# Instance norm in 3D: tiles of 48 KiB per partition in four slots, with masked sums and some stores on the load queue

## The chip, the core and the metric

The kernel runs on one core of a Trainium2 chip. Five engines are used: VectorE (DVE), ScalarE (ACT), TensorE (PE), GpSimd (POOL) for the set-up, and SyncE (SP), which issues loads. Transfers between HBM and the on-chip memory (SBUF, 128 partitions) are issued on queues of SP and ACT and carried by 16 DMA engines that all queues share. The metric is the device time of one execution in microseconds, as the median of the runs; less is better.

## The reference

Each of 8 x 64 = 512 instances (one batch entry and one channel) has 32 x 64 x 64 = 131072 float32 values. Each is normalised by its own mean and variance:

```
mean = np.mean(x, axis=(2, 3, 4), keepdims=True)
var = np.var(x, axis=(2, 3, 4), keepdims=True)
return ((x - mean) / np.sqrt(var + eps)).astype(np.float32)
```

The input is 268.4 MB, and so is the output; each value must be read once and written once.

## The kernel before

**Tiles.** A tile is 128 partitions x 8192 columns, 32 KiB per partition, 4 MiB, contiguous in HBM. It holds 8 instances, 16 partitions each. There are 64 tiles; the last is taken as two halves of 4096 columns per partition. Six tile buffers (`slots`) of 32 KiB per partition take turns: tile k is in slot k % 6. `LANES` = 8 sets of semaphores, small buffers and PSUM banks serve six slots and two halves.

**Engines.** Every engine has its own instruction stream, written out in order; semaphores connect them, and there is no scheduler. `over_tiles` runs one engine's `step` over ten rounds of six tiles (a hardware loop) and then over the rest, three tiles and two halves. For one tile:

- `on_vector` (DVE): sums the left half of the columns (L79), later adds the two sums out of PSUM with the sign turned, which is minus the mean (L82), takes the reciprocal of the root (L89), makes the shift (L92), and scales and shifts the right half in place (L95).
- `on_scalar` (ACT): sums the right half (L107), squares the whole tile around the mean with a running sum (L113), takes the root of the variance plus eps (L120), scales and shifts the left half in place (L123), and issues the store of the tile (L130) when both halves are done.
- `on_tensor` (PE): two matmuls with a constant 128 x 128 matrix `avg` that adds the 16 partitions of an instance and divides by 131072 (L136 for the sums, L143 for the squares).

The outputs of L107 and L113 themselves are thrown away (`unused`, one byte per element); only their sums count.

**Queues.** `load_all` (SP) issues six loads at once (L180); then, in a loop, the load of each further tile waits until the store of the tile that had the slot has landed (L185, and L192 for the rest). All stores are on ACT's queue, behind the work of their tile in ACT's stream. A queue's transfers are carried in order of issue. At the end ACT waits for all stores.

**Set-up.** GpSimd builds `avg` (for 8 and for 4 instances) with a memset (L201) and masks (L204), and the constant eps (L214); ACT and PE wait for it.

Of the kernel before, what the change touches and what calls it, by code (L numbers as in the profile page):

```python
# [9 lines left out]
def kernel(  # L10
# [17 lines left out]
    COLS = 8192  # L28
    SLOTS = 6
    FULL = P * COLS // n_elem  # L30
    n_tiles = n_inst // FULL
    ROUNDS = (n_tiles - 1) // SLOTS
    LANES = SLOTS + 2

    x_f = x.rearrange("b c d h w -> (b c) (d h w)")
    out_f = out.rearrange("b c d h w -> (b c) (d h w)")
    x_t = x_f.rearrange("(k i) (s f) -> k (i s) f", i=FULL, s=P // FULL)
    out_t = out_f.rearrange("(k i) (s f) -> k (i s) f", i=FULL, s=P // FULL)
    x_h = x_f.rearrange("(k i) (s f) -> k (i s) f", i=FULL // 2, s=2 * P // FULL)
    out_h = out_f.rearrange("(k i) (s f) -> k (i s) f", i=FULL // 2, s=2 * P // FULL)  # L40

    ctx.enter_context(tc.tile_critical(name="norm"))  # L42

    def sbuf(name, shape, dtype=fp32):
# [4 lines left out]
    unused = sbuf("unused", [P, COLS], mybir.dt.uint8)  # L49
    eps_t = sbuf("eps_t", [P, 1])  # L50
    avg = {n: sbuf(f"avg{n}", [P, P]) for n in (FULL, FULL // 2)}
    small = [sbuf(f"small{i}", [P, 8]) for i in range(LANES)]
    psum = [
        ctx.enter_context(nc.psum_tensor(f"psum{i}", [P, 512], fp32))
        for i in range(LANES)
    ]

    def semaphores(name, n):
        return [ctx.enter_context(nc.semaphore(f"{name}{i}")) for i in range(n)]

    ready = semaphores("ready", 1)[0]
    landed = semaphores("landed", LANES)
    summed = semaphores("summed", LANES)
    meaned = semaphores("meaned", LANES)
    centred = semaphores("centred", LANES)
    squared = semaphores("squared", LANES)
    varied = semaphores("varied", LANES)
    rooted = semaphores("rooted", LANES)
    scaled = semaphores("scaled", LANES)
    shifted = semaphores("shifted", LANES)  # L70
    done = semaphores("done", LANES)
    stored = semaphores("stored", LANES)
# [3 lines left out]
    def on_vector(eng, t, lane, n, c1, c2, c16):  # L76
        w = t.shape[1] // 2
        a = small[lane]
        eng.reduce_sum(  # L79
            out=a[:, 0:1], in_=t[:, :w], axis=mybir.AxisListType.X  # L80
        )._wait_ge(landed[lane], c16).then_inc(summed[lane], 1)
        eng.tensor_reduce(  # L82
            out=a[:, 2:3],
            in_=psum[lane][:, 0:2],
            axis=mybir.AxisListType.X,
            op=Alu.add,
            negate=True,
        )._wait_ge(meaned[lane], c1).then_inc(centred[lane], 1)
        eng.reciprocal(out=a[:, 5:6], in_=a[:, 4:5])._wait_ge(  # L89
            rooted[lane], c1  # L90
        ).then_inc(scaled[lane], 1)
        eng.tensor_mul(out=a[:, 6:7], in0=a[:, 2:3], in1=a[:, 5:6])._wait_ge(  # L92
            scaled[lane], c1
# [4 lines left out]
            scalar1=a[:, 5:6],  # L98
            scalar2=a[:, 6:7],
            op0=Alu.mult,  # L100
            op1=Alu.add,
        )._wait_ge(shifted[lane], c1).then_inc(done[lane], 1)

    def on_scalar(eng, t, lane, n, c1, c2, c16, dst):
        w = t.shape[1] // 2
        a = small[lane]
        eng.activation(  # L107
            out=unused[:, w : 2 * w],
            in_=t[:, w:],
            func=Act.Identity,  # L110
            accum_out=a[:, 1:2],
        )._wait_ge(landed[lane], c16).then_inc(summed[lane], 1)
        eng.activation(  # L113
            out=unused[:, : 2 * w],
# [4 lines left out]
        )._wait_ge(centred[lane], c1).then_inc(squared[lane], 1)  # L119
# [7 lines left out]
            scale=a[:, 5:6],  # L127
            bias=a[:, 6:7],
        )._wait_ge(shifted[lane], c1).then_inc(done[lane], 1)
        eng.dma_start(out=dst, in_=t)._wait_ge(done[lane], c2).then_inc(  # L130
            stored[lane], 16
        )

# [131 lines left out]
```

## Time and profile before

| what | value |
|---|---|
| median of 3 runs | 1248.04 us (1247.95 to 1248.22) |
| the profiled execution: its own time | 1247.95 us |
| its span in the profile | 1246.2 us |
| instructions in the span | 1808 |
| bytes moved | 536.90 MB, 431 GB/s over the span |
| share of the chain that ended last | ACT 48%, DVE 29% |
| DVE's idle time before L79, ended by a load | 163.7 us in 53 waits |
| ACT's idle time before L107, ended by a load | 76.7 us in 44 waits |
| activation table loads | 20, of 1283 ns each |

The page has the busy time of each engine, the span in 40 slices (a digit is the busy share in tenths), the DMA queues with their packets (q1 carries what SP issues, q10 what ACT issues), the chain of work that ended last, the groups of instructions by line, and the DMA issues with their time to landing. In a group the shape is out<-in, then the count, busy time and the mean of one, and the idle time before them with what ended it. Idle time of an engine that does not set the end costs nothing.

### The profile page before, as it was taken

How to read it: one execution, taken by the hardware profiler on the slowest of the kernel's cores; microseconds unless marked ns; L12 is line 12 of the kernel's file. 1: busy time of each engine (PE TensorE's matmuls, PEld its weight loads, DVE VectorE, ACT ScalarE, POOL GpSimd, SP SyncE). 2: the span in 40 equal slices, each digit the busy share in tenths (PEclk: the TensorE clock that was granted, in tenths of full speed). 3: DMA queues.
4: the chain of work that ended last, by engine and by line, in shares of the span. 5: the costliest groups of instructions: out<-in, count | busy, mean ns of one | idle time of the engine just before them, and what ended most of it. 6: DMA issues, size and time to landing. Idle time of an engine off the chain costs nothing.

```text
span 1246.2 us, 1808 instructions
## 1 busy us (share of the span) xinstructions
PE 76.4 (6%) x260; PEld 65.2 (5%) x260; DVE 468.0 (38%) x325; ACT 986.1 (79%) x410; POOL 1.9 (0%) x11
## 2 busy tenths in 40 slices
PE   0000000000000000000000000000000000000000
PEld 0000000000000000000000000000000000000000
DVE  2344334433334334343343433434334333343331
ACT  5888888887787878778777877787787778878774
POOL 0000000000000000000000000000000000000000
DMA  9999999999999999999999999999999999999998
GB/s 404 421 438 428 430 438 436 428 431 438 435 429 431 438 435 429 431 436 436 429 431 436 436 429 430 438 436 426 433 438 436 426 433 438 435 425 435 438 429 380
DMA packets 18722, 536.90 MB, mean 431 GB/s; under 512 B 2080, under 2 KB 2080, under 8 KB 2080
## 3 DMA queue, kind: packets, MB, share of 16 engines
q1 hardware_dynamic: 9360, 268.44, 50.0%
q10 hardware_dynamic: 9360, 268.44, 49.9%
q14 instruction: 2, 0.02, 0.0%
HBM read 268.44 MB, written 268.44 MB: 431 GB/s over the span
## 4 chain that ended last, share of the span: by engine, by line
ACT 48%; DVE 29%; another core or an unknown queue 13%; PE 6%; issue 1%; DMA 1%; ACTq 0%; DVEq 0%; SPq 0%
ACT unused L113 37%; DVE small L79 18%; DVE slot L95 8%; ACT slot L123 4%; ACT unused L107 4%; PE psum L136 3%; PE psum L143 3%; ACT small L120 1%; ACT L120 1%; DMA slot<-in_x_dram 1%; DVE small L89 1%; DVE small L82 1%; DVE small L92 1%; ACTq L130 0%
## 5 line engine op out<-in xcount | busy, mean ns | idle before, releaser
L113 ACT ACTIVATE unused<-slot,small 128x8192 uint8<-128x8192 f32 (+1 forms) x65 | 456.1, 7016 | 90.2 <-DVE small L82 90.2
L79 DVE TENSOR_REDUCE small<-slot 128x1 f32<-128x4096 f32 (+1 forms) x65 | 283.0, 4353 | 163.7 <-DMA slot<-in_x_dram 163.7
L107 ACT ACTIVATE unused<-slot 128x4096 uint8<-128x4096 f32 (+1 forms) x65 | 231.7, 3564 | 81.9 <-DMA slot<-in_x_dram 76.7
L123 ACT ACTIVATE slot<-slot,small 128x4096 f32<-128x4096 f32 (+1 forms) x65 | 243.7, 3749 | 27.6 <-DVE small L92 27.6
L89 DVE RECIPROCAL small<-small 128x1 f32<-128x1 f32 x65 | 10.6, 164 | 533.8 <-ACT small L120 533.8
L95 DVE TENSOR_SCALAR slot<-slot,small 128x4096 f32<-128x4096 f32 (+1 forms) x65 | 154.7, 2380 | 2.4
L136 PE MATMUL psum<-small,avg 128*128 128x2 f32 x130 | 38.2, 363 | 673.9 <-DVE small L79 548.5
L136 PEld LDWEIGHTS psum<-small,avg 128*128 128x128 f32 x130 | 32.6, 311 | 679.4 <-DVE small L79 552.7
L143 PE MATMUL psum<-small,avg 128*128 128x1 f32 x130 | 38.2, 363 | 480.6 <-ACT unused L113 480.6
L143 PEld LDWEIGHTS psum<-small,avg 128*128 128x128 f32 x130 | 32.7, 312 | 486.1 <-ACT unused L113 486.1
L120 ACT ACTIVATE small<-psum,eps_t 128x1 f32<-128x1 f32 x65 | 17.0, 261 | 37.4 <-PE psum L143 37.3
L82 DVE TENSOR_REDUCE small<-psum 128x1 f32<-128x2 f32 x65 | 10.4, 160 | 62.8 <-PE psum L136 62.8
L107 ACT ACT_TABLE_LOAD x10 | 12.8, 1283 | 10.4 <-ACT slot L123 7.1
L120 ACT ACT_TABLE_LOAD x10 | 12.8, 1283 | 0.2
L107 ACT ACTIVATION_READ_ACCUMULATOR unused<-slot 128x1 f32 x65 | 12.1, 186 | 0.0
L113 ACT ACTIVATION_READ_ACCUMULATOR unused<-slot,small 128x1 f32 x65 | 12.1, 186 | 0.0
L92 DVE TENSOR_TENSOR small<-small 128x1 f32<-128x1 f32 x65 | 10.4, 159 | 2.2
L204 POOL TENSOR_SCALAR_AFFINE_SELECT avg<-avg 128x128 f32<-128x128 f32 x4 | 1.3, 324 | 0.3
L201 POOL MEMSET avg<- 128x128 f32 x2 | 0.4, 204 | 0.5 <-SPq L42 0.5
L246 POOL MEMSET const-bfloat16-1.0<- 128x1 bf16 x1 | 0.1, 101 | 0.0
L246 POOL MEMSET const-uint8-127<- 128x1 uint8 x1 | 0.1, 101 | 0.0
L214 POOL MEMSET eps_t<- 128x1 f32 x1 | 0.1, 99 | 0.0
(2 smaller groups left out, 0.2 us busy)
## 6 DMA issues: line engine op xcount, KB each, us to landing
slot<-in_x_dram SPq DMA_DIRECT2D x63, 4096.0 KB, 53.3
out_dram<-slot ACTq DMA_DIRECT2D x63, 4096.0 KB, 45.3
slot<-in_x_dram SPq DMA_DIRECT2D x2, 2048.0 KB, 55.6
out_dram<-slot ACTq DMA_DIRECT2D x2, 2048.0 KB, 14.7
```

Source lines behind the costliest of these rows:

```text
L79: eng.reduce_sum(out=a[:, 0:1], in_=t[:, :w], axis=mybir.AxisListType.X)._wait_ge(landed[lane], c16).then_inc(summed[lane], 1)
L82: eng.tensor_reduce(out=a[:, 2:3], in_=psum[lane][:, 0:2], axis=mybir.AxisListType.X, op=Alu.add, negate=True,)._wait_ge(meaned[lane], c1) ...
L89: eng.reciprocal(out=a[:, 5:6], in_=a[:, 4:5])._wait_ge(rooted[lane], c1).then_inc(scaled[lane], 1)
L92: eng.tensor_mul(out=a[:, 6:7], in0=a[:, 2:3], in1=a[:, 5:6])._wait_ge(scaled[lane], c1).then_inc(shifted[lane], 1)
L95: eng.tensor_scalar(out=t[:, w:], in0=t[:, w:], scalar1=a[:, 5:6], scalar2=a[:, 6:7], op0=Alu.mult, op1=Alu.add,)._wait_ge(shifted[lane], ...
L107: eng.activation(out=unused[:, w : 2 * w], in_=t[:, w:], func=Act.Identity, accum_out=a[:, 1:2],)._wait_ge(landed[lane], c16).then_inc(sum ...
L113: eng.activation(out=unused[:, : 2 * w], in_=t, func=Act.Square, bias=a[:, 2:3], accum_out=a[:, 3:4],)._wait_ge(centred[lane], c1).then_in ...
L120: eng.activation(out=a[:, 4:5], in_=psum[lane][:, 2:3], func=Act.Sqrt, bias=eps_t[:, 0:1])._wait_ge(varied[lane], c1).then_inc(rooted[lane ...
L123: eng.activation(out=t[:, :w], in_=t[:, :w], func=Act.Identity, scale=a[:, 5:6], bias=a[:, 6:7],)._wait_ge(shifted[lane], c1).then_inc(don ...
L136: eng.matmul(out=psum[lane][:, 0:2], lhsT=avg[n][:], rhs=a[:, 0:2], start=True, stop=True,)._wait_ge(summed[lane], c2).then_inc(meaned[lan ...
L143: eng.matmul(out=psum[lane][:, 2:3], lhsT=avg[n][:], rhs=a[:, 3:4], start=True, stop=True,)._wait_ge(squared[lane], c1).then_inc(varied[la ...
L204: eng.affine_select(out=m[:], in_=m[:], pattern=[[sign * split, n], [0, split]], compare_op=Alu.is_ge, fill=0.0, base=0 if sign < 0 else s ...
```

## The change

Tiles become 12288 columns wide, 48 KiB per partition and 6 MiB, in four slots. A tile is made of three chunks of 4096 columns. Since an instance is 32 chunks, a partition can hold the end of one instance and the start of the next. 512 instances are 128 parts of 128 x 4096 columns; two parts (2 MiB each) come first, then 41 tiles, then three parts.

- **Sums by masks.** Each chunk has its own sum. `over_instance` turns the sums per chunk into sums per instance: DVE multiplies the sums of a partition's chunks with a mask `belongs` (which chunk belongs to which of up to three groups of the partition), PE adds over partitions with `avg`, DVE reduces out of PSUM, multiplies with the mask again and reduces, which gives a value per chunk. This is done twice for a tile, for the means and for the variances.
- **Work of a tile.** DVE sums the first chunk and the last 1536 columns; ACT sums the second chunk and 2560 columns of the third. DVE subtracts the mean from the first chunk in place and squares and sums it in one instruction; ACT squares and sums the other two. DVE scales chunk 0 and scales and shifts chunk 1; ACT does chunk 2.
- **Parts.** A part is worked as a half tile was before (`part_on_vector`, `part_on_scalar`, `part_on_tensor`), without a store on ACT.
- **Queues.** On SP: two part loads, the load of tile 0, the store of part 0, the load of tile 1, the store of part 1, the loads of tiles 2 and 3 (which wait for the stores of the parts that lay in their slots), and then the loop. At the end SP issues the load of tile 40, three part loads (into the three chunks of one slot, after the store of tile 37), the store of tile 40 and the stores of the three parts, and waits for all stores. Tiles 0 to 39 are stored on ACT's queue as before.
- **Set-up.** GpSimd builds `within` and `belongs` besides `avg` (for one size); DVE waits for it too. ACT loads the activation table that has the root once, ahead of all.

The diff, cut to its core:

```diff
-    COLS = 8192
-    SLOTS = 6
-    FULL = P * COLS // n_elem
-    n_tiles = n_inst // FULL
-    ROUNDS = (n_tiles - 1) // SLOTS
-    LANES = SLOTS + 2
+    CHUNK = 4096
+    THIRDS = 3
+    COLS = THIRDS * CHUNK
+    SLOTS = 4
+    PART = P * CHUNK // n_elem
+    FRONT = 2
+    n_tiles = (n_inst // PART - FRONT) // THIRDS - 1
+    n_parts = n_inst // PART - THIRDS * n_tiles
+    ROUNDS = n_tiles // SLOTS
+    LANES = SLOTS + n_parts
...
+    def over_instance(eng, a, p, at, m, to, negate, c1, wait, steps):
+        n = THIRDS
+        by_both = at + m
+        by_instance = by_both + n * m
+        by_chunk = by_instance + n
+        eng.tensor_tensor(
+            out=block(a, by_both, n, m),
+            in0=spread(a, at, m),
+            in1=belongs[:, :, :m],
+            op=Alu.mult,
+        )._wait_ge(*wait).then_inc(steps[0], 1)
         eng.tensor_reduce(
...
+            out=a[:, by_instance : by_instance + n],
+            in_=p.rearrange("p (n m) -> p n m", m=m),
+            axis=AXIS,
             op=Alu.add,
...
+        )._wait_ge(steps[1], c1).then_inc(steps[2], 1)
+        eng.tensor_tensor(
+            out=block(a, by_chunk, n, n),
+            in0=spread(a, by_instance, n),
+            in1=belongs[:, :, :n].rearrange("p i c -> p c i"),
+            op=Alu.mult,
+        )._wait_ge(steps[2], c1).then_inc(steps[3], 1)
+        eng.tensor_reduce(
+            out=a[:, to : to + n],
+            in_=block(a, by_chunk, n, n),
+            axis=AXIS,
+            op=Alu.add,
+            negate=negate,
+        )._wait_ge(steps[3], c1).then_inc(steps[4], 1)
...
+    def tile_on_vector(eng, t, lane, c1, c3, c4, c16):
+        a, p = small[lane], psum[lane]
+        chunk = [t[:, i * CHUNK : (i + 1) * CHUNK] for i in range(THIRDS)]
+        for j, part in ((0, chunk[0]), (3, t[:, COLS - TURN :])):
+            eng.reduce_sum(out=column(a, SUMS, j), in_=part, axis=AXIS)._wait_ge(
+                landed[lane], c16
+            ).then_inc(summed[lane], 1)
+        over_instance(
+            eng, a, p[:, 0:12], SUMS, 4, MEANS, True, c1, (summed[lane], c4),
+            (sorted_[lane], meaned[lane], joined[lane], picked[lane], centred[lane]),
+        )
+        eng.tensor_scalar(
+            out=chunk[0],
+            in0=chunk[0],
+            scalar1=column(a, MEANS, 0),
+            scalar2=None,
+            op0=Alu.add,
+        )._wait_ge(centred[lane], c1).then_inc(moved[lane], 1)
+        eng.tensor_tensor_reduce(
+            out=unused[2][:],
+            in0=chunk[0],
+            in1=chunk[0],
+            scale=1.0,
+            scalar=0.0,
+            op0=Alu.mult,
+            op1=Alu.add,
+            accum_out=column(a, SQUARES, 0),
+        )._wait_ge(moved[lane], c1).then_inc(squared[lane], 1)
+        over_instance(
+            eng, a, p[:, 12:21], SQUARES, 3, VARS, False, c1, (squared[lane], c3),
...
+    def tile_on_scalar(eng, t, lane, c1, c3, c4, c16, dst):
...
+        for j, part in ((1, chunk[1]), (2, chunk[2][:, : CHUNK - TURN])):
+            eng.activation(
+                out=unused[j - 1][:, : part.shape[1]],
+                in_=part,
+                func=Act.Identity,
+                accum_out=column(a, SUMS, j),
+            )._wait_ge(landed[lane], c16).then_inc(summed[lane], 1)
+        for j in (1, 2):
+            eng.activation(
+                out=unused[j - 1][:],
+                in_=chunk[j],
+                func=Act.Square,
+                bias=column(a, MEANS, j),
+                accum_out=column(a, SQUARES, j),
+            )._wait_ge(centred[lane], c1).then_inc(squared[lane], 1)
...
+        if dst is not None:
+            eng.dma_start(out=dst, in_=t)._wait_ge(done[lane], c3).then_inc(
+                stored[lane], 16
+            )
...
     def load_all(eng):
+        def part(m):
+            lane, t, slot, uses = parts[m]
+            load = eng.dma_start(out=t, in_=part_of(x_f, m))
+            if uses:
+                load._wait_ge(stored[slot], 16 * uses)
+            load.then_inc(landed[lane], 16)
+
+        def store_part(m):
+            lane, t, _, _ = parts[m]
+            eng.dma_start(out=part_of(out_f, m), in_=t)._wait_ge(done[lane], 2).then_inc(
+                stored[lane], 16
+            )
+        for m in range(FRONT):
+            part(m)
         for s in range(SLOTS):
-            eng.dma_start(out=slots[s][:], in_=x_t[s]).then_inc(landed[s], 16)
+            load = eng.dma_start(out=slots[s][:], in_=x_t[s])
+            if s >= SLOTS - FRONT:
+                load._wait_ge(stored[s + FRONT], 16)
+            load.then_inc(landed[s], 16)
+            if s < FRONT:
+                store_part(s)
...
+        for k in range(ROUNDS * SLOTS, n_tiles):
+            eng.dma_start(out=slots[k % SLOTS][:], in_=x_t[k])._wait_ge(
+                stored[k % SLOTS], 16 * (k // SLOTS)
+            ).then_inc(landed[k % SLOTS], 16)
+        for m in range(FRONT, n_parts):
+            part(m)
+        s = TAIL % SLOTS
+        eng.dma_start(out=out_t[TAIL], in_=slots[s][:])._wait_ge(
+            done[s], 3 * (TAIL // SLOTS + 1)
+        ).then_inc(stored[s], 16)
+        for m in range(FRONT, n_parts):
+            store_part(m)
...
+    nc.vector.wait_ge(ready, set_by)
...
+    nc.scalar.preload_act_table(Act.Sqrt)
     nc.scalar.wait_ge(ready, set_by)
```

`TURN` is 1536, `TAIL` is 40 (the last tile), and `parts` lists lane, buffer, slot and the slot's stores to wait for, for each of the five parts. `block`, `spread` and `column` are views of a small buffer of 72 columns per lane. The two halves of `over_instance` use semaphores of their own.

## The prediction

> **What bounds the kernel now.** I read the page first: busy shares, the 40 slices, the DMA queues.
>
> ```profile
> PE 76.4 (6%) x260; PEld 65.2 (5%) x260; DVE 468.0 (38%) x325; ACT 986.1 (79%) x410; POOL 1.9 (0%) x11
> DMA  9999999999999999999999999999999999999998
> GB/s 404 421 438 428 430 438 436 428 431 438 435 429 431 438 435 429 431 436 436 429 431 436 436 429 430 438 436 426 433 438 436 426 433 438 435 425 435 438 429 380
> q1 hardware_dynamic: 9360, 268.44, 50.0%
> q10 hardware_dynamic: 9360, 268.44, 49.9%
> ```
>
> ScalarE (ACT) is busy 79% of the span, but the two DMA queues together fill 99.9% of the 16 DMA engines' time. Each queue has 63 x 128 packets of 32 KiB (one per partition of a tile), 2 x 128 of 16 KiB and 65 x 16 small packets that close a transfer: 9360.
>
> Next the windows, to see whether the mix of loads and stores matters. Columns: stretch, its length, five engines' busy time, clock, DMA share, GB/s.
>
> ```profile
> 6.00:30.20 24.20, 1.18 (x4) 1.01 (x4) 7.36 (x6) 14.92 (x7) 0.00 (x0) 1.00 1.00 433
> 200.00:1168.25 968.25, 59.11 (x202) 50.55 (x202) 365.70 (x250) 772.32 (x318) 0.00 (x0) 1.00 1.00 433
> 1236.00:1242.07 6.07, 0.00 (x0) 0.00 (x0) 0.00 (x0) 0.00 (x0) 0.00 (x0) 1.00 1.01 432
> ```
>
> Loads alone, both directions, and 16 KiB stores alone all give 432 to 433 GB/s. One queue fills the engines as well as two do. So the end is set by bytes, plus what a packet costs beyond its bytes, plus any time in which neither queue has work.
>
> Last the queues: the issues (size, median us to landing) and the loads' waits.
>
> ```profile
> slot<-in_x_dram SPq DMA_DIRECT2D x63, 4096.0 KB, 53.3
> out_dram<-slot ACTq DMA_DIRECT2D x63, 4096.0 KB, 45.3
> SPq L185 <- DMA out_dram<-slot: 1048.9, 54, 50.6
> ```
>
> Loads wait for free slots, not slots for loads. A tile's load and store take 19.4 us of the engines, and a load lands 53.3 us after its issue, so 34 us of other work stands before it. 53.3 + 45.3 + some 17.5 us of compute is 116 us, six slots at 19.4.
>
> **DMA work, the term that counts.** Bytes stay at 536.87 MB. In the trace's packet records, followed start to start on one DMA engine, a 32 KiB packet takes 1.2094 us and a 16 KiB packet 0.6073. The difference, 0.6021 us, is what 16 KiB cost; 5.2 ns are left per packet. By the windows' rounded rates that remainder lies between 0 and 6 ns. A 48 KiB packet is not in the trace; on the same line it takes 1.8115.
>
> Before, an engine has 63 x 8 x 2 = 1008 large and 32 small data packets. After, it has 41 x 8 x 2 = 656 of 48 KiB and 5 x 8 x 2 = 80 of 16 KiB: 304 fewer, at 5.2 ns, -1.58 us (0 to -1.82 by the windows). Closing packets fall from 130 to 92. On an ordinary engine the records show 6 ns for one, -0.23 us. But a transfer is complete when its slowest engine is, and tiles start every 19.39 us (L107 at 1135.94 and 1155.33 in the timeline), while 16 x 1.2094 is 19.35: 0.04 us per pair of transfers. Nineteen pairs fewer at that price are -0.76. I take -0.5, the middle. Sum -2.1 us, if the engines stay filled.
>
> The Trainium skill, "DMA: Bandwidth & Descriptors", section "Why small descriptors are slow (HBM only)", gives a fixed cost of about 3 cycles per packet and dates it to this chip; with the page's 850 MHz that is an estimate of 3.5 ns, 304 of them are 1.07 us, and the time would be 1246.5 by it. The records' 5.2 ns decide.
>
> **Compute, which must stay inside 29.0 us per tile.** A 48 KiB tile needs 16 x 1.8115 + 0.04 = 29.0 us of the engines. The rows, by form (busy us, mean ns):
>
> ```profile
> L113 ACT ACTIVATE unused<-slot,small 128x4096 uint8<-128x4096 f32 x2 | 7.4, 3707 | 2.0 <-DVE small L82 2.0
> L79 DVE TENSOR_REDUCE small<-slot 128x1 f32<-128x4096 f32 x63 | 278.4, 4419 | 162.0 <-DMA slot<-in_x_dram 162.0
> L79 DVE TENSOR_REDUCE small<-slot 128x1 f32<-128x2048 f32 x2 | 4.6, 2282 | 1.7 <-DMA slot<-in_x_dram 1.7
> L123 ACT ACTIVATE slot<-slot,small 128x4096 f32<-128x4096 f32 x63 | 239.5, 3801 | 26.8 <-DVE small L92 26.8
> L107 ACT ACTIVATE unused<-slot 128x4096 uint8<-128x4096 f32 x63 | 227.8, 3617 | 80.5 <-DMA slot<-in_x_dram 75.8 <-ACT slot L123 4.6
> L107 ACT ACTIVATE unused<-slot 128x2048 uint8<-128x2048 f32 x2 | 3.8, 1910 | 1.3 <-DMA slot<-in_x_dram 0.9 <-ACT slot L123 0.4
> L95 DVE TENSOR_SCALAR slot<-slot,small 128x4096 f32<-128x4096 f32 x63 | 152.0, 2413 | 2.3
> ```
>
> Sums: ACT 3.62 for the middle chunk, 1.91 + 512 x 0.833 ns = 2.34 for 2560 columns, two accumulator reads at 0.19: 6.33. VectorE (DVE) 4.42 + (2.28 - 512 x 1.043 ns) = 6.17. Group step: product, matmul, two reductions, product: four small ops at 0.16 (L82, L92), 0.68 for the matmul (the idle time before L82), some 0.2 of handovers: 1.5. Centred squares: ACT 2 x (3.71 + 0.19) = 7.79; DVE subtracts in 2.41, then the fused square and sum. No such row exists. Below it cannot be under the 2.41 of L95; above, two passes of L79, 8.84. It reads and accumulates as L79 does, so 4.42 + 0.19: 7.0 in all, under ACT. Second group step 1.5, Sqrt 0.3, reciprocal and product 0.36, two DVE scalings 4.83 (ACT's 3.80 beside them), store issue 0.34, further handovers 0.4. Sum 23.4 us; at the upper bound 27.0; at the lower 23.4 still. All are under 29.0, so the sums by masks cost nothing as long as the DMA covers them: the cover is 5.6 us, and without it every us is paid 41 times. The 20 table loads that go (1.28 us each) and the lighter ACT pay nothing either, for the same reason.
>
> **Slots.** Four at 29.0 give the same 116 us. Load 29.0, compute 23.4 and store 29.0 at half rate leave 34 us of queueing (before: 116 - 38.8 - 17.5 = 60). Thinner, but neither queue empties.
>
> **The moved stores and the start.** On SP, two part loads, tile 0's load, then the store of part 0, which waits for its result; behind it in SP stand tile 1's load, part 1's store and tiles 2 and 3. The first tile was computed from 13.23, after 4 MiB; part 0 is 2 MiB, 4.8 us less: 8.4. A half tile takes 10.4 us:
>
> ```profile
> 1223.26 1.91 ACT L107 ACTIVATE unused<-slot 128x2048 uint8<-128x2048 f32 x1 [0.93 <-DMA slot<-in_x_dram]
> 1233.70 0.34 ACTq L130 DMA_DIRECT2D out_dram<-slot  x1
> ```
>
> So part 0's store and tile 1's load are issued near 19, while tile 0's load keeps the engines filled until 12.9 + 14.5 = 27.4: 8 us of cover. Part 1's store comes near 29. Part 0's store moves behind tile 0, ends at 32.3 and frees tile 2's load at about 34, while tile 1 runs to 47 and part 1's store to 52. No gap. The longer set-up on GpSimd (about nine more small ops, 0.1 to 0.3 us each, after 2.99) is over by about 5.5, before 8.4; if not, the 8 us still cover it.
>
> The Trainium skill, "Perfetto Trace Analysis", section "DMA Optimizations", speaks against this: one engine should issue inputs, another outputs. Were the 8.5 and 17 us that the two part stores stand behind loads lost, the time would be 1271; the window of loads alone at 433 GB/s says they are not.
>
> **The end.** From the last whole tile's landing: 0.4 + 23.4, three parts at 10.4, 1.0 from issue to first packet: 56 us to the last store's start. Meanwhile the engines owe three part loads (14.6), stores of tiles 39 and 40 (29.0), two part stores (9.7) and the rest of tile 38's store (half rate, some 3): 56.3. This balances with nothing to spare; I take 0, with 0 to +5 for the range, 4.9 being the last store moved by itself.
>
> **How the sum stands.** The profiled execution took 1247.95 us, its span 1246.2, so 1.75 lie outside; the median 1248.04 is 0.09 above it. Span after 1244.1; 1248.04 - 2.1 = 1245.9.
>
> **Rivals.**
> Faster, 1244.7: the packet records end on one DMA engine at 1244.67 and on most at about 1243, a lag of 1.5 us. If it goes with the fewer transfers, 1.58 + 0.23 + 1.5 = 3.3 are saved. For it: the lag grows with each transfer (19.39 against 19.36 on the others). Against: it may be that engine's own.
> Split rows, 1249.3: the change doesn't make 48 KiB packets, each row going as two. 656 more packets at 5.2 ns are +3.4 on the forecast. For it: no packet above 32 KiB is seen. Against: 16 and 32 KiB rows both go whole.
> Slower, 1251.4: the last tile and the three parts outlast the DMA's backlog. If the fused square and sum takes two passes (+3.6) and the eight small ops of a tile take 0.4 instead of 0.16 (+1.9), the chain is 61.5 us against 56.3: +5.2, a little more than the last store. It decides as soon as the chain exceeds what the engines owe then. Against: a later store leaves the engines to the loads, so that more is owed at that point. Beyond 29.0 per tile the same cause would cost 41 us per us.
>
> **Chances and range.** Forecast 0.55, faster rival 0.25, split 0.06, slower 0.14. A measurement of this kernel tells 0.2%, 2.5 us, from no change: limits 1245.54 and 1250.54. The forecast's own bounds (packets 0 to 1.82, closing packets 0.23 to 0.76) are 1245.5 to 1247.8, and the runs before spread over 0.27 us; with the lower limit only 0.4 us under the forecast, I put a fifth of it (0.12) below. So faster 0.37, same 0.43 + 0.06 = 0.49, slower 0.14. The range 1244.4 to 1249.6 leaves out the slower rival and a bit below.
>
> **What would show it.** Packets per queue 6624; DMA slices 9 throughout; SP's waits on stores still long; DVE idle before its sums on the load; the fused square and sum near 4.4 us; no table load in the loop. Wrong would be: a DMA slice under 9 before the last, a tile cadence other than 29.0, over 6624 packets, or a rate below 433 in the middle.

## The result, and the profile after

| | before | after |
|---|---|---|
| median | 1248.01 us (the runs beside the change) | 1397.01 us (1393.07, 1399.53, 1404.35, 1394.48) |
| ratio | | 1.12, 95% interval 1.115 to 1.1251 |
| profiled execution, its span | 1247.95, 1246.2 us | 1393.07, 1391.3 us |
| idle time of one DMA engine, mean of 16 | 2.1 us | 93.5 us |
| packets' time beyond their usual length, per DMA engine | 1.5 us | 56.7 us |
| load packets, store packets over 5% longer than usual | 0.4%, 0% | 18%, 15% |

The forecast was 1245.9 us. The last three rows of the table come from the trace's packet records: for each size the commonest record is "usual" (1.815 us for 48 KiB), what a record has beyond it is "stretch", and idle is the time in which a DMA engine has no packet. The page of after first (span, engines, 40 slices, queues, issues):

```profile
span 1391.3 us, 1977 instructions
...
PE 55.0 (4%) x184; PEld 46.0 (3%) x184; DVE 804.5 (58%) x722; ACT 764.0 (55%) x441; POOL 2.7 (0%) x15
...
DMA  9999999899999999999999899999999999998957
GB/s 398 426 424 420 431 427 393 365 386 404 384 383 386 384 384 384 384 398 389 384 384 387 362 387 404 384 384 384 384 384 384 403 386 384 386 401 367 374 240 327
...
q1 hardware_dynamic: 7488, 285.22, 49.0%
q10 hardware_dynamic: 5760, 251.66, 44.3%
...
slot<-in_x_dram SPq DMA_DIRECT2D x41, 6144.0 KB, 64.9
out_dram<-slot ACTq DMA_DIRECT2D x40, 6144.0 KB, 43.4
```

Here the fault is seen at once, and also where it is not. The packets are as forecast (7488 + 5760 is 2 x 6624) and no engine is near full, but the rate falls from 425 to some 384 GB/s after five or six slices and stays there. The load's median time from issue to landing, 64.9 us, is kept in mind for a comparison further on. The slices' 9s hide the idle time, since a 9 is anything from 90%.

The waits of after, with what ended them (total us, times, longest):

```profile
ACT unused L215 <- DMA slot<-in_x_dram: 456.8, 39, 14.5
DVE small L159 <- DMA slot<-in_x_dram: 428.1, 40, 13.8
...
```

ACT waited 76.7 us for loads in all before, and waits 456.8 now: 11.7 in each of 39 tiles. One tile on ACT, out of the timeline (start, duration):

```profile
614.75 3.62 ACT L215 ACTIVATE unused<-slot 128x4096 uint8<-128x4096 f32 x1 [11.39 <-DMA slot<-in_x_dram]
...
636.65 0.34 ACTq L243 DMA_DIRECT2D out_dram<-slot  x1
647.56 3.62 ACT L215 ACTIVATE unused<-slot 128x4096 uint8<-128x4096 f32 x1 [11.69 <-DMA slot<-in_x_dram]
```

From the first sum to the store's issue are 21.9 us; the next tile starts 32.8 us after this one. The compute is shorter than the 23.4 of the forecast. It is the tile that comes late. And the windows, at the end of this tile, over the middle and near the end (length, five engines' busy time, clock, DMA share, GB/s):

```profile
300.00:1180.00 880.00, 32.30 (x108) 27.00 (x108) 516.80 (x460) 476.00 (x273) 0.00 (x0) 1.00 0.94 387
630.00:634.00 4.00, 0.59 (x2) 0.50 (x2) 2.84 (x7) 2.23 (x2) 0.00 (x0) 1.00 0.92 393
634.00:637.00 3.00, 0.00 (x0) 0.00 (x0) 2.62 (x2) 1.87 (x1) 0.00 (x0) 1.00 0.14 49
1335.00:1353.00 18.00, 1.20 (x4) 1.00 (x4) 15.27 (x17) 14.51 (x11) 0.00 (x0) 1.00 0.13 54
```

Over the middle, where before has 433 GB/s at a share of 1.00, the DMA has 387 at 0.94. Inside each tile there is a hole: from 634 to 637, just ahead of the store's issue at 636.65, the DMA is 14% busy. Two of sixteen engines at work are 12.5%. The packet records show two packets under way at 636, both of the load queue and one of them of 2.75 us; the other fourteen engines have none. The records of the loads' semaphores (16 increments, one per engine) say how far the engines are apart: for tile 8 the first comes at 242.8 us and the last at 288.7, 46 us apart, and ACT starts the tile at 288.72; before, 0.3 to 2.1 us lie between first and last. The spread grows from the start: 7 us for tile 2, then 13, 18, 29, 38 and 44, and it stays at 44 to 46.

The Trainium skill, "DMA: Bandwidth & Descriptors", section "Why a DMA increments its semaphore by 16 and not by 1", says that the engines of one transfer finish independently, and that only the full count of 16 means that all data has landed. The 46 us agree. A tile lands when its slowest engine is done, so a packet that is late on one engine is paid by all sixteen.

The time is thereby accounted for: 56.7 - 1.5 = 55.2 us more stretch and 93.5 - 2.1 = 91.4 us more idle time are 146.6; the profiled execution is 147.2 over the forecast. What was open is what stretches the packets: 48 KiB rows, four slots, the compute, the stores on the load queue at the start, or those at the end.

### The profile page after: what moved, and what is told of

It reads as the page before. It is cut to its first block, busy times and chain, and to the rows that moved or that the text cites. A ratio compares the mean times of both kernels' runs of the same rounds, so it can differ in the third digit from the quotient of the medians.

```text
span 1391.3 us, 1977 instructions
## 1 busy us (share of the span) xinstructions
PE 55.0 (4%) x184; PEld 46.0 (3%) x184; DVE 804.5 (58%) x722; ACT 764.0 (55%) x441; POOL 2.7 (0%) x15
## 3 DMA queue, kind: packets, MB, share of 16 engines
q1 hardware_dynamic: 7488, 285.22, 49.0%
q10 hardware_dynamic: 5760, 251.66, 44.3%
## 4 chain that ended last, share of the span: by engine, by line
DVE 35%; another core or an unknown queue 31%; ACT 26%; PE 4%; issue 3%; DMA 1%; DVEq 0%; ACTq 0%; SPq 0%
ACT unused L222 22%; DVE small L159 17%; DVE slot L202 7%; DVE slot L195 5%; PE psum L253 4%; ACT unused L292 1%; DVE small L139 1%; DVE small L127 1%; DVE small L133 1%; DVE small L145 1%; ACT small L229 1%; ACT unused L215 1%; ACT slot L302 1%; DMA slot<-in_x_dram 1%
## 5 line engine op out<-in xcount | busy, mean ns | idle before, releaser
L159 DVE TENSOR_REDUCE small<-slot 128x1 f32<-128x4096 f32 x82 | 249.3, 3081 | 428.1 <-DMA slot<-in_x_dram 428.1
L215 ACT ACTIVATE unused<-slot 128x4096 uint8<-128x4096 f32 x82 | 243.3, 2968 | 458.0 <-DMA slot<-in_x_dram 456.8
L222 ACT ACTIVATE unused<-slot,small 128x4096 uint8<-128x4096 f32 x82 | 303.4, 3701 | 63.7 <-DVE small L145 63.7
L173 DVE CUSTOM_DVE_ANT_0 unused<-slot 128x4096 uint8<-128x4096 f32 x41 | 181.5, 4426 | 1.4
L235 ACT ACTIVATE slot<-slot,small 128x4096 f32<-128x4096 f32 x41 | 155.9, 3801 | 18.1 <-DVE small L190 18.1
L253 PE MATMUL psum<-small,avg 128*128 128x9 f32 (+1 forms) x164 | 49.1, 375 | 1271.9 <-DVE small L127 1271.9
L202 DVE TENSOR_SCALAR slot<-slot,small 128x4096 f32<-128x4096 f32 x41 | 98.7, 2407 | 0.0
L166 DVE TENSOR_SCALAR slot<-slot,small 128x4096 f32<-128x4096 f32 x41 | 96.5, 2353 | 1.5
L195 DVE TENSOR_SCALAR slot<-slot,small 128x4096 f32<-128x4096 f32 x41 | 96.2, 2347 | 0.0
L253 PEld LDWEIGHTS psum<-small,avg 128*128 128x128 f32 x164 | 41.0, 311 | 1279.9 <-DVE small L127 1279.9
L133 DVE TENSOR_REDUCE small<-psum 128x3 f32<-128x12 f32 x82 | 13.8, 169 | 56.7 <-PE psum L253 56.7
L127 DVE TENSOR_TENSOR small<-small,belongs 128x12 f32<-128x12 f32 x82 | 13.9, 170 | 30.9 <-ACT unused L222 28.8
L292 ACT ACTIVATE unused<-slot,small 128x4096 uint8<-128x4096 f32 x5 | 18.5, 3708 | 5.7 <-DVE small L269 5.7
L139 DVE TENSOR_TENSOR small<-small,belongs 128x9 f32<-128x9 f32 x82 | 13.9, 170 | 2.8
## 6 DMA issues: line engine op xcount, KB each, us to landing
slot<-in_x_dram SPq DMA_DIRECT2D x41, 6144.0 KB, 64.9
```

Of the source, the lines that this page charges most:

```text
L127: eng.tensor_tensor(out=block(a, by_both, n, m), in0=spread(a, at, m), in1=belongs[:, :, :m], op=Alu.mult,)._wait_ge(*wait).then_inc(steps ...
L139: eng.tensor_tensor(out=block(a, by_chunk, n, n), in0=spread(a, by_instance, n), in1=belongs[:, :, :n].rearrange("p i c -> p c i"), op=Alu ...
L159: eng.reduce_sum(out=column(a, SUMS, j), in_=part, axis=AXIS)._wait_ge(landed[lane], c16).then_inc(summed[lane], 1)
L166: eng.tensor_scalar(out=chunk[0], in0=chunk[0], scalar1=column(a, MEANS, 0), scalar2=None, op0=Alu.add,)._wait_ge(centred[lane], c1).then_ ...
L173: eng.tensor_tensor_reduce(out=unused[2][:], in0=chunk[0], in1=chunk[0], scale=1.0, scalar=0.0, op0=Alu.mult, op1=Alu.add, accum_out=colum ...
L195: eng.tensor_scalar(out=chunk[0], in0=chunk[0], scalar1=column(a, SCALES, 0), scalar2=None, op0=Alu.mult,)._wait_ge(scaled[lane], c1).then ...
```

## The experiments

### First: transfers alone, and each size by itself

Theory R held that rows of 48 KiB stretch by themselves; the rivals were the four slots, the compute's timing, and the mixed load queue. The first kernel is the change without any arithmetic: its output is its input, and each store waits for its load alone. Edits here are against the change unless it is said.

```diff
 def tile_on_scalar(eng, t, lane, c1, c3, c4, c16, dst):
...
-            eng.dma_start(out=dst, in_=t)._wait_ge(done[lane], c3).then_inc(
+            eng.dma_start(out=dst, in_=t)._wait_ge(landed[lane], c16).then_inc(
```

> The change's transfers alone: tiles of 48 KiB per partition, four slots, the same queues and order, and each store waits for its load instead of the results; all computing is left out, so the output is the input. Theory R (the 48 KiB rows themselves are what one DMA engine moves slowly): packets over 2 us stay and the time is near 1390 us, above 1330 at least. Theory C (the new work of VectorE and ScalarE on the same memory slows the DMA): all packets near 1.815 us and some 1244 us. Theory S (four slots with computing between load and store leave the DMA engines too little queued work): near 1244 us too, since a store now follows its load at once; a lagging engine may be seen but costs little.

Measured: 1359.55 and 1383.16 us, too far apart for a ratio. The 40 slices of the run of 1383.16:

```profile
GB/s 389 419 422 428 423 433 430 431 434 428 417 411 406 401 403 403 397 384 381 371 377 371 380 374 377 377 370 370 383 373 374 381 366 380 370 366 381 366 380 214
```

It runs at some 420 to 430 for ten slices, falls, and stays at 370 to 380. So no compute is needed: the transfers of the change, in their order, do this by themselves.

The second is the same with the kernel before (`COLS = 8192`, `SLOTS = 6`, stores waiting for their loads, no arithmetic).

> The same for the kernel before: 32 KiB per partition, six slots, all computing left out, the output is the input. Every theory expects 1246 to 1249 us and packets of 1.21 us; it is the measure for the copy of 48 KiB rows. If it is slower, copying without pauses is itself disturbed and that copy must be read against this one.

Measured: 1247.43 us, ratio 1.0005 (0.998 to 1.003). The packets of before don't stretch even so.

The third has the change's compute and queues with each tile moved as three transfers of 16 KiB per partition, the fifth as two of 24 KiB:

```diff
+    def move(eng, dst, src, up, behind=None, count=None):
+        w = COLS // 3
+        for i in range(3):
+            d = eng.dma_start(
+                out=dst[:, i * w : (i + 1) * w], in_=src[:, i * w : (i + 1) * w]
+            )
+            if behind is not None and i == 0:
+                d._wait_ge(behind, count)
+            d.then_inc(up, 16)
...
-                eng.dma_start(out=slots[s][:], in_=x_t[it * SLOTS + s])._wait_ge(
-                    stored[s], c16
-                ).then_inc(landed[s], 16)
+                move(eng, slots[s][:], x_t[it * SLOTS + s], landed[s], stored[s], c16)
```

> The change with each tile's load and store issued as three transfers of 128 x 16 KiB (one per chunk) instead of one of 128 x 48 KiB; tiles, slots, computing and output as in the change. Theory R: packets of 0.61 us, the slow engine is gone, and the time is 1242 plus 1312 more data packets per engine at 5.2 ns, about 1253 us, under 1280 at any rate. Theories C and S: the slow packets only become shorter, the loss stays, 1370 to 1410 us.

> The change with each tile's load and store issued as two transfers of 128 x 24 KiB. Theory L (packets above 32 KiB are what goes wrong): packets of 0.91 us and about 1251 us (352 more data packets per engine than before at 5.2 ns, 22 more pairs of transfers at 0.04 us). Theory N (rows that are no power of two go wrong): slow packets again, above 1300 us.

Measured: 1255.07 us (1.0061, 1.0038 to 1.0083) and 1252.38 us (1.0035, 1.0019 to 1.0051). Both are over 140 us better than the change with the same compute, slots, order of issue and queues. So neither the compute nor the slots nor a store on the load queue is enough to spoil it. I took this for proof of R. It wasn't, as will be seen.

The fourth is the kernel before with fewer slots:

```diff
-    SLOTS = 6
+    SLOTS = 4
```

> The kernel before with four slots of 32 KiB instead of six, nothing else. A round of the slots is 4 x 19.4 = 77.6 us, of which load, store and computing take 38.8 + 17.5. Theory S: with 21 us of queueing left the same lag appears and the time rises by more than 5%, above 1310 us. Theories R and C: 1248 to 1256 us.

Measured: 1249.77 us, 1.001 (0.9999 to 1.0021). Four slots of 32 KiB hold a third less than the change's 192 KiB per partition, and the queues stay full.

Then only the stores, or only the loads, in three transfers (`move` of above on one side):

> The change with only the tiles' stores issued as three transfers of 16 KiB rows; loads stay whole, 48 KiB rows. Theory W (the 48 KiB stores are slow, the loads only wait behind them): about 1250 us, load packets at 1.815 us. Theory B (either direction suffices): above 1290 us with slow load packets.

> The change with only the tiles' loads issued as three transfers of 16 KiB rows; stores stay whole. Theory W: the time stays above 1340 us, with stores of 2.4 us and more. Theory B: above 1290 us. If the loads alone are at fault: about 1250 us.

Measured: 1294.44 us (1.0372, 1.0342 to 1.0402) and 1286.45 us (1.0308, 1.0147 to 1.0469). Both lie between; the second is the median of 1277.98 and 1294.91, too far apart to tell more than that it is slower. In the second the 16 KiB loads are stretched too, by 18.4 us per engine, beside 48 KiB stores. A small row next to a stretched one is not safe, which R alone doesn't say.

### Second: rows of other sizes, all stores on one queue

Copies with nothing but loads on one queue and stores on the other, for rows of 40, 44, 48 and 64 KiB. The first three leave out the end of the data, which doesn't fill a tile (0.4%, 1.2% and 1.6%). The edit, for 48 KiB, is against the kernel before:

```diff
-    COLS = 8192
-    SLOTS = 6
+    COLS = 12288
+    SLOTS = 4
+    n_tiles = n_inst * n_elem // (P * COLS)
...
+    for k in range(n_tiles):
+        s, uses = k % SLOTS, k // SLOTS
+        load = nc.sync.dma_start(out=slots[s][:], in_=x_t[k])
+        if uses:
+            load._wait_ge(stored[s], 16 * uses)
+        load.then_inc(landed[s], 16)
+        nc.scalar.dma_start(out=out_t[k], in_=slots[s][:])._wait_ge(
+            landed[s], 16 * (uses + 1)
+        ).then_inc(stored[s], 16)
```

(`COLS = 10240`, `SLOTS = 5`; `COLS = 11264`, `SLOTS = 4`; `COLS = 16384`, `SLOTS = 3` for the others.)

> A plain copy in tiles of 40 KiB per partition, five slots, 51 tiles (the last 2048 columns' worth, 0.4% of the data, and all computing are left out). Packets that go as those before would take 1.510 us and a pair of tiles 24.2 us, 1237 us in all. Theory L: slow packets, above 1270 us. Theory T (48 KiB is special, by its pitch or as the size that one engine can't hold, 40 is not): 1235 to 1242 us.

> The same in 46 tiles of 44 KiB per partition, four slots (1.2% of the data and all computing are left out). Clean: packets of 1.661 us, 46 x 26.6 + 6, about 1231 us. Theory L2 with its bound between 40 and 44 KiB: above 1270 us; with its bound between 44 and 48 KiB, or theory P: 1228 to 1236 us.

> A plain copy in 42 tiles of 48 KiB per partition from the start of the tensor, four slots, no parts, no stores on the load queue (4 MiB, 1.6% of the data, and all computing are left out). Clean packets would give 42 x 29.0 + 6, about 1225 us. Theory L2 (packets of 48 KiB are too long, wherever they lie): slow packets and above 1270 us. Theory P (it takes the parts ahead of the tiles, their 4 MiB offset, or their stores on the load queue): 1222 to 1230 us.

> The same in 32 tiles of 64 KiB per partition, three slots, all of the data; all computing is left out. Clean packets would be 2.414 us (or 1.21, were a row cut in two) and the time 32 x 38.7 + 6, about 1244 us. Theory L2: at least as slow as 48 KiB in proportion, above 1300 us. Theory P, or 48 KiB as a special pitch: 1240 to 1250 us.

Measured: 1242.70 us (40 KiB), 1231.76 (44), 1226.76 (48) and 1255.17 (64, runs from 1249.43 to 1259.45; 1.0053, 0.9988 to 1.0118). The slices of the 48 KiB copy:

```profile
GB/s 385 437 435 435 437 429 435 429 433 435 437 435 435 427 432 437 437 430 435 433 435 430 432 435 437 437 437 430 433 433 437 427 435 435 437 437 433 432 435 387
```

Here are 42 tiles in 48 KiB rows through four slots, at full rate to the end, and the time is what the forecast's packet price gives: 42 x 8 x 2 packets an engine by 1.8115 are 1217.3 us, and 9.4 are left. Before it is 1008 x 1.2094 + 32 x 0.6073 = 1238.5 us, and 9.5 are left. R falls. Large rows aren't the cause, and 48 KiB packets have their forecast price.

Last of this set, the change with all its stores on ACT's queue:

```diff
+        eng.dma_start(out=part_of(out_f, lane - SLOTS), in_=t)._wait_ge(
+            done[lane], 2
+        ).then_inc(stored[lane], 16)
...
-            if s < FRONT:
-                store_part(s)
...
-        for m in range(FRONT, n_parts):
-            store_part(m)
```

> The change with its queue move undone: the five parts and the last tile are stored on ScalarE's queue like all others; rows, slots, computing and output as in the change. Theory L2: the loss stays, 1370 to 1410 us. Theory P, as far as it lies in stores on the load queue: about 1246 us.

Measured: 1252.92 us, 1.0036 (1.0016 to 1.0056). 144 us of the loss are gone with the moved stores. What it keeps over before is idle time at the end (9.3 us an engine): the last store stands behind ACT's other work and is issued at 1245.39.

### Third: which of the moved stores

Only the first two parts' stores on ACT's queue; only the last tile's and the last three parts'; and the first of these with SP still waiting where it waits in the change, but without issuing a store there:

```diff
+        if lane - SLOTS < FRONT:
+            eng.dma_start(out=part_of(out_f, lane - SLOTS), in_=t)._wait_ge(
+                done[lane], 2
+            ).then_inc(stored[lane], 16)
...
             if s < FRONT:
-                store_part(s)
+                eng.wait_ge(done[SLOTS + s], 2)
```

(front_on_act has the same without the `if` and the wait; tail_on_act has `lane - SLOTS >= FRONT` instead, leaves SP's stores of the first two parts alone and takes those of the end from it.)

> The change with only the first two parts stored on ScalarE's queue; the last tile and the last three parts stay on the load queue. Theory F (the first two stores on the load queue bring the DMA engines out of step, and they stay so): clean packets of 1.815 us and 1245 to 1248 us, the change's forecast. Theory E (the stores at the end): still above 1370 us.

> The reverse: only the last tile and the last three parts are stored on ScalarE's queue, the first two parts stay on the load queue. Theory F: still above 1370 us, slow packets from the first tiles on. Theory E: about 1252 us, as with all of them moved.

> As front_on_act, but SyncE waits after tile 0's load until part 0 is done, and after tile 1's load until part 1 is done, as it does in the change to issue their stores. So the loads come as late as in the change, but no store stands between them. Theory F by order in the queue (a store between loads of one queue): 1245 to 1250 us. Theory F by delay (too little work queued at the start): above 1350 us.

> The change itself, unaltered, beside its variants on one chip. Every theory that puts the loss into the kernel expects 1380 to 1410 us again; if the loss belongs to one chip, it would be some 1246 us here.

| stores of the first two parts | stores of the end | median us | ratio to before |
|---|---|---|---|
| load queue | load queue (the change again) | 1402.02 | 1.1232 (1.12 to 1.1265) |
| load queue | ACT | two runs, 1263.85 and 1399.22 | no ratio |
| ACT | load queue | 1248.67 | 1.0003 (0.9992 to 1.0015) |
| ACT, SP waits as in the change | load queue | 1250.55 | 1.0012 (1.0001 to 1.0024) |

With the first two parts' stores on ACT's queue the loss is gone, though the stores of the end stay on the load queue. So the first two bring it on, and the end's do no harm. Nor is it SP's waiting that does it. tail_on_act bears this out only in part: over 1370 us was expected of it, and the run that has a trace took 1263.85, 15.7 over before. Up to the stores of the end it does what the change does, so the two stores make the loss possible, but don't fix its size. The slices and issues of front_on_act, and its window over the middle:

```profile
DMA  9999999999999999999999999999999999999997
GB/s 393 431 429 438 438 433 430 429 443 433 433 430 435 438 432 433 430 436 438 433 430 429 440 436 433 430 430 438 438 433 429 435 440 430 435 429 438 428 436 339
...
slot<-in_x_dram SPq DMA_DIRECT2D x41, 6144.0 KB, 39.0
out_dram<-slot ACTq DMA_DIRECT2D x40, 6144.0 KB, 55.0
...
300.00:1180.00 880.00, 35.88 (x120) 29.98 (x120) 576.29 (x511) 530.96 (x301) 0.00 (x0) 1.00 1.00 434
```

and a tile of it in the timeline:

```profile
625.44 3.62 ACT L215 ACTIVATE unused<-slot 128x4096 uint8<-128x4096 f32 x1 [7.94 <-DMA slot<-in_x_dram]
...
647.34 0.34 ACTq L243 DMA_DIRECT2D out_dram<-slot  x1
654.52 3.62 ACT L215 ACTIVATE unused<-slot 128x4096 uint8<-128x4096 f32 x1 [7.96 <-DMA slot<-in_x_dram]
```

The same 21.9 us of compute, but tiles 29.08 us apart (the forecast: 29.0), and loads that land 39.0 us after their issue instead of 64.9.

### Fourth: how two stores that are over by 53 us spoil the next 1300

A DMA engine carries 8 packets of each tile. While both queues have work, loads and stores share it, and a tile takes 8 pairs of packets (3.62 us a pair). So the place of the load in its tile, against that of the store in its own, set once, stays as long as both queues have work and their packets keep step. I call it the offset: the time from the start of a tile's store to the start of the next load, in pairs of packets; 8 is 0 again. The packet records of the first tiles (start in us, median of the 16 engines):

```
                 load of tile 2   store of tile 0   load of tile 3   offset
the change            52.30            55.83             81.41         7.1
front_on_act          49.81            63.15             74.03         3.0
```

In front_on_act the part stores stand ahead of tile 0's store in ACT's queue and hold it until 63.15. In the change they went with the loads, nothing is ahead of tile 0's store, and it starts 3.5 us after the load of tile 2: the two run almost side by side through their tiles. The theory of the offset says that this is what stretches the packets. All kernels, sorted by it:

| kernel | offset | load, store packets over 5% longer | stretch, idle (us per engine) | median us |
|---|---|---|---|---|
| before, four slots | 2.0 | 0.8%, 0% | 2.4, 2.7 | 1249.77 |
| front_on_act | 3.0 | 0.5%, 0.2% | 2.1, 4.5 | 1248.67 |
| front_on_act_held | 3.0 | 0.9%, 0.3% | 2.6, 6.4 | 1250.55 |
| all stores on ACT (e12) | 3.0 | 0.6%, 0.5% | 2.5, 9.3 | 1252.92 |
| copy of before (e2) | 4.1 | 0.5%, 0% | 1.5, 0.8 | 1247.43 |
| copy, 40 KiB | 5.0 | 0.8%, 0% | 2.1, 2.5 | 1242.70 |
| change in 3 x 16 KiB | 5.0 | 0.4%, 0% | 1.8, 2.9 | 1255.07 |
| copy, 48 KiB | 5.8 | 1.4%, 0% | 2.5, 1.4 | 1226.76 |
| copy, 44 KiB; change in 2 x 24 KiB; before | 6.0 | 0.3 to 0.7%, 0% | 1.5 to 2.0, 2.1 to 4.0 | 1231.76; 1252.38; 1248.04 |
| copy, 64 KiB | 7.0, slides to 4.8 | 4.9%, 0.2% | 6.4, 7.4 | 1255.17 |
| tail_on_act (the run of 1263.85) | 7.0 to 7.1 | 10.7%, 0.2% | 12.5, 8.6 | two runs |
| the change, and again | 7.1, 7.1, 7.4, then the engines part | 18%, 15%; 11%, 12% | 56.7, 93.5; 45.2, 115.2 | 1397.01; 1402.02 |
| copy of the change (e1, the run of 1383.16) | 0.9, 7.4, 2.2 to 2.5, then slides to 0.1 | 20%, 29% | 88.7, 51.6 | 1359.55, 1383.16 |

(In the two runs with one side in three, loads and stores have packets of different lengths, and the offset doesn't stay.) Where it stays between 2.0 and 6.0, hardly a packet is stretched (1.4% of the loads at most); every kernel at 7.0 to 0.9 has more. The runs that seemed to speak for R, in 16 and 24 KiB rows, start a load as long after the store as the change does, some 25.4 us. But a tile has 24 or 16 of their packets on an engine, and the load is 21 or 14 pairs behind the store, 3 or 2 short of the same place; 5.0 and 6.0 say this in the measure of 8. So at one and the same delay in microseconds the size of the packets does matter.

The trace of e1 crosses the range within one execution of one program. From 100 to 350 us its offset is 2.2 to 2.5, and 1% of the stores are stretched; then it slides, and from 750 to 1300 us it is 0.1 to 0.3, and 42% are:

```profile
100.00:350.00 250.00, 0.00 (x0) 0.00 (x0) 1.00 1.00 429
750.00:1300.00 550.00, 0.00 (x0) 0.00 (x0) 1.00 0.96 374
```

(Here the busy times are ACT's and POOL's alone.) At 7.0 to 7.1 the outcome is open. In the trace of tail_on_act the offset holds there to the end, with one load in nine stretched and 430 GB/s in the middle; in the change, whose transfers are the same up to the end, the engines part within five tiles. What tips it isn't shown.

The table and these traces were read after the fact, so the last two runs set the offset by hand. One more load (half the partitions of a tile, 32 KiB each, 2 MiB: four packets an engine, 4.84 us by the packet price) goes into the load queue after tile 1's load, into columns of slot 3 that tile 3 writes later. In the change it should make 7 into 3, in front_on_act 3 into 7 or more:

```diff
+        def fill():
+            eng.dma_start(
+                out=slots[SLOTS - 1][:64, CHUNK:], in_=x_t[0][:64, CHUNK:]
+            ).then_inc(filled, 16)
...
+            if s == SLOTS - 1:
+                eng.wait_ge(filled, 16)
             load = eng.dma_start(out=slots[s][:], in_=x_t[s])
...
+            if s == FRONT - 1:
+                fill()
```

> The change, stores on the load queue and all, with one extra load of 64 partitions x 32 KiB (4 packets on each DMA engine, 2 MiB, 4.9 us, its data unused) between the store of part 1 and the load of tile 2. Theory O (the loss needs load and store streams of a DMA engine less than a packet pair or so from the same place in their tiles): the load of tile 2 comes some 3 pairs after the store's start instead of 7.3, the packets stay at 1.815 us and the time is 1246 + 5 to 9, so 1250 to 1258 us. Theory M (a store between loads in one queue, whatever the offset): still above 1370 us.

> front_on_act, which was clean at an offset of 3.0, with the same extra load at the same place in the load queue, and no store in that queue until the end. Theory O: the offset becomes 7.0 and packets are stretched as in the change or as in tail_on_act, 1262 us or more in at least some runs. Theory M: 1249 + 5, so 1252 to 1256 us, clean.

Measured: the change with 2 MiB more to carry takes 1270.62 us (1.018, 1.016 to 1.02) instead of 1397 to 1402, and the good kernel with the same 2 MiB 1449.48 us (1.1615, 1.1582 to 1.1648) instead of 1248.67. The middle of the two (the window of the shifted change, then of shifted front_on_act with its slices):

```profile
300.00:1180.00 880.00, 35.96 (x120) 30.07 (x120) 573.59 (x511) 528.33 (x301) 0.00 (x0) 1.00 1.00 429
```

```profile
GB/s 397 382 373 371 372 379 371 374 363 372 367 374 372 370 366 375 368 371 367 368 368 378 370 372 375 372 381 375 372 364 376 368 376 378 379 387 370 370 349 314
```

```profile
300.00:1300.00 1000.00, 35.34 (x118) 29.54 (x118) 564.20 (x501) 519.80 (x297) 0.00 (x0) 1.00 0.99 373
```

The offset of the first was 3.2 and 3.0 for two tiles, as wanted, then it jumped; from there on it is 6.6 to 7.0, with 13% of the loads stretched, hence 1270.62 and not the 1250 to 1258 expected. The jump comes from the compute. Tile 2 came later by the added load, and its store could not be issued before its results were there:

```profile
97.68 3.62 ACT L216 ACTIVATE unused<-slot 128x4096 uint8<-128x4096 f32 x1 [25.15 <-DMA slot<-in_x_dram]
...
119.57 0.34 ACTq L244 DMA_DIRECT2D out_dram<-slot  x1
```

The store of tile 1 had ended at 113.5, and this one's packets start at 123.46, 7.5 us later than they would have 29.0 us after the store before. For so long the loads had the engines to themselves, at 1.81 us a packet, and gained four packets. Of the 143 us that the change lies over 1253.5 (1248.67 and the added 4.84), 126 are gone. The offset of the second was meant as 7 and is 8.4 to 9.0 for 26 tiles, that is 0.4 to 1.0 (then it slides to 6.6). It is at some 373 GB/s from the third slice on with its DMA engines 99% busy: 32% of the loads and 65% of the stores are stretched, by 174.9 us per engine, with 27.4 idle. There is no store in its load queue up to the end. So it isn't the mixing of stores with loads, nor the waits of SP, nor the added load, which made one kernel faster and the other slower; the loss follows the offset.

## Why the prediction was wrong, point by point

**What bounds the kernel: half right.** Bytes and packets bound it, as it said. But "end is set by bytes, plus what a packet costs beyond its bytes, plus any time in which neither queue has work" leaves out a fourth term: a packet can take over twice its time, 3.8 us for 1.815. Three windows of before at 432 to 433 GB/s were read as a rate that any mix of loads and stores has. They show it for loads alone, stores alone, and one offset, 6.0.

**Packets: right.** 2 x 6624 in all, though not 6624 in each queue, since the moved stores count on the load queue; 48 KiB start to start 1.8117 us in an undisturbed stretch, against 1.8115. The saving of 2.1 us was there, but the good version doesn't keep it: front_on_act has 0.6 us more stretch and 2.4 us more idle time than before, 3.0 in all. Less 2.1 that is +0.9; measured is +0.53 against the runs beside it, which is within the noise.

**Compute: right.** The fused square and sum and the other groups of after, by form:

```profile
L173 DVE CUSTOM_DVE_ANT_0 unused<-slot 128x4096 uint8<-128x4096 f32 x41 | 181.5, 4426 | 1.4
...
L127 DVE TENSOR_TENSOR small<-small,belongs 128x12 f32<-128x12 f32 x41 | 7.0, 171 | 2.0 <-ACT unused L215 0.6
```

4.43 us where 4.42 was taken from L79, small operations at 0.17 where 0.16 was, and 21.9 us a tile to the issue of the store against 23.4. The sums by masks cost nothing, since the DMA covers them: front_on_act does all of them in 1248.67. The set-up grew by four operations on GpSimd (15 against 11 on the page), not by about nine.

**Four slots: right, with a good offset.** That "neither queue empties" holds in front_on_act (share 1.00 over the middle) and fails in the change (0.94), as the effect of late tiles.

**The moved stores and the start: this step failed.** Its times were right: SP's issues of after, by the timeline (forecast: near 19, 29 and 34):

```profile
19.32 0.34 SPq L377 DMA_DIRECT2D out_dram<-slot  x1
...
29.34 0.34 SPq L377 DMA_DIRECT2D out_dram<-slot  x1
33.96 19.80 SPq L386 DMA_DIRECT2D slot<-in_x_dram  x2
```

There is "No gap" at the start, as it said, and a cost of nothing would follow if moved work cost only what it takes itself. The price stands elsewhere. Where the two stores are queued sets how the load stream stands to the store stream for the tiles to come: an offset of 7.1 in the change against 3.0 without the move. That was worth 1397.01 - 1248.67 = 148 us. Three of the prediction's signs of being wrong came: slices under 9, 32.8 us a tile, and 387 GB/s in the middle. I asked of the moved stores what is late next, found nothing late, and stopped.

The Trainium skill's advice that was weighed there ("Perfetto Trace Analysis", "DMA Optimizations": one engine for inputs, another for outputs) would have put the time on the right side, though the 1271 made of it was a delay at the start that didn't come. The page says only that it may make sense, "to allow more dynamic spread", and the last run shows that following it is no protection: loads and stores apart up to the end, and 1449.48.

**The end: nearly right.** The forecast took 0, with 5 us as a bound; front_on_act, which keeps that end, has 4.5 us of idle time in all, 2.4 more than before. In the change the last tile comes late, and from 1335 to 1353, until its store can be issued, the engines have little left to carry (13%).

**Rivals.** The split rows are refuted (rows of 48 and 64 KiB go whole, 1.815 and 2.418 us). The faster rival has no support: front_on_act, clean and with as few transfers, saves nothing. The slower rival named the right sign and the wrong mechanism (and its 1251.4 should be 1251.1, the forecast and its own +5.2). The range ended where the known mechanisms ended.

## What to carry to other kernels

In these kernels, where two queues keep the DMA engines full, the time also depends on where one stream stands against the other, and a transfer added or moved at the start shifts that for many tiles. Read the rate in the middle of the run after every change to the head of a queue, and if it fell, look at how far the 16 increments of one transfer's semaphore lie apart. A full rate in the profile of before vouches for that alignment alone; an experiment on sizes must keep the offset, counted in packets, or it tests two things.

## What had not been expected of the hardware

- Loads and stores of one tile size share the DMA engines at 430 to 434 GB/s at offsets from 2.0 to 6.0 of 8 packets, at 429 to 430 at 6.6 to 7.1 as long as the engines stay together, and at 371 to 374 at 0.1 to 1.0.
- Near 7 it looks unstable: the same program (tail_on_act) took 1263.85 and 1399.22 us (the second without a trace), and the change parts its engines within five tiles.
- Still open: what two streams at the same place in their tiles collide on (the same partitions of SBUF, or addresses in HBM) wasn't tried; nor whether the 32 KiB rows of before would suffer at an offset near 0; nor what tips a kernel at 7.1. The change's own two stores were not run at an offset that stays good, in 48 KiB rows. No version tried beats the kernel before by what can be measured.
